# Half the depth of the mixing's output projection by Strassen's seven block products, in a two-layer decoder trunk

## The chip, the cores and the metric

The kernel runs on one core of one Trainium2 chip, as one launch. The time is device time in microseconds (us), lower is better; given is the median of several runs, and the runs of before agree within 0.01%. A profiled execution is a run of its own, with its own time.

## The reference

Two layers; in each a half-step SwiGLU block, a mixing of three attentions, and a second half-step SwiGLU block, each between RMSNorms. SEQ is 512, D_MODEL 1024, all in float32. The mixing ends with a product of two matrices, 512x1024 by 1024x1024:

```python
for l in range(DEPTH):                      # 2
    f = _swiglu(_rmsnorm(h, ffn1_pre_g[l]), ffn1_w_gate[l], ffn1_w_up[l], ffn1_w_down[l])
    h = h + 0.5 * _rmsnorm(f, ffn1_post_g[l])
    u = _rmsnorm(h, mix_pre_g[l])
    ...
    merged = (g_sb * (_merge_heads(o_sb) @ w_br_sb[l])
              + g_fx * (_merge_heads(o_fx) @ w_br_fox[l])
              + g_mem * (_merge_heads(o_mem) @ w_br_mem[l]))
    h = h + _rmsnorm(merged @ w_out[l], mix_post_g[l])
    f = _swiglu(_rmsnorm(h, ffn2_pre_g[l]), ffn2_w_gate[l], ffn2_w_up[l], ffn2_w_down[l])
    h = h + 0.5 * _rmsnorm(f, ffn2_post_g[l])
```

## The kernel before

**Numbers in two parts.** TensorE multiplies fp32r, a shortened float32. To keep float32's accuracy each operand is split into a high part (a cast on ScalarE, ACT, line 188) and a low part (what is left, on VectorE, DVE, line 189), and each product is three matmuls: high by high, low by high, high by low (`mm3`, lines 214 to 216). A matmul here multiplies a 128x128 piece by a 128x512 piece and adds into one PSUM bank of 128x512. A weight comes as a pair of row tiles: a load on SP's queue into a slot `raw_...` (line 262, 512 KB), the cast to `wh_...`, the low part `wl_...`.

**The SwiGLU blocks** use seven block products for eight (Strassen's scheme, in Winograd's variant) already. `block_units` makes the weights of the products. Three of the seven need sums of weight blocks: `BlockUnit.fetch` (L317) loads one block on SP and lets POOL issue a second DMA that adds the other block to it in SBUF; for products 3 and 6, `load` adds a further block on DVE (L343). The products' results are collected in three pairs of PSUM banks, and `product` hands them on: ACT copies a bank to the rows (L963), DVE adds a bank to them.

**The mixing** (`mixing`) works feature-major: `merge(br, ...)` forms a gate and a branch's projection for two of the eight 128-feature tiles at a time and adds them up in `merged` (tiles `mg`, four of 128x2x512). Its last four calls (branch 1, `dp` 0 to 3) finish two features tiles each, and split each at once into `ms_0` to `ms_7`, the left factors of the output projection.

**The output projection** is `down(w_out[l], ND, ...)`, with tiles named `wo` and `pwo`. It has 8 row tiles of weights (k-tiles) by 4 token tiles by 2 column halves by 3 passes, 192 matmuls a layer. `down` runs in this order: `first` does column half 0 of token tiles 0 and 1 side by side; `late` does half 1 of tile 0, then of tile 1; `second` half 1 of tiles 2 and 3; `late` half 0 of tile 2, then of tile 3. After each half `dst.result` takes the squares of the bank for the norm on ACT (`sq`, L554) and the scaled copy to the rows `f` on DVE (L559). When a tile is whole, `Q.spawn(dst.chain(t))` starts its chain: the norm (L505 to L510, on DVE and ACT), the addition to the residual `hm` (L596), the next norm, and at last four transposes per half on TensorE (`utb`, L613), whose results are the left factors of the next SwiGLU block. Its first weights (`tc`) are loaded in `first` too (`marks["next"]`).

**What sets the order.** The program is written through a queue of jobs, `Q`: a job is a list of weights to load and a generator that emits TensorE work, and `step` loads the weights of later jobs ahead (`AHEAD` = 4). Chains are woven into the jobs by a modelled clock (`PE_US`). The engines then take their instructions in the order in which they were written: each engine strictly in turn, and the loads in turn on SP's queue, the adding DMAs in turn on POOL's. With `carry=True`, which before only the SwiGLU blocks use, `down` seeds a bank with what stands in the rows already (`seed`, L1086, an ACT copy into PSUM), and its matmuls add to that:

```python
AFTER = {(0, 0): ((0, 1),), (0, 1): ((1, 1),), (1, 1): ((2, 1), (3, 1)), (2, 1): ((2, 0),), (2, 0): ((3, 0),)}
```

Of the kernel before, what the change touches and what calls it, by code (L numbers as in the profile page):

```python
# [9 lines left out]
F32 = mybir.dt.float32  # L10
# [3 lines left out]
ALU = mybir.AluOpType  # L14
# [3 lines left out]
P = 128  # L18
# [4 lines left out]
def kernel(  # L23
# [38 lines left out]
    nc = tc.nc  # L62
# [45 lines left out]
    def blk(tag, name):  # L108
        return stile([P, 2, S], tag, name)
# [525 lines left out]

    HR = 8 * ("o",)
    ORDER = (0, 2, 3, 4, 5, 1, 6)
    FIRST = (0, 1, 2, 3, 4, 5, 6)

    def ffn(l, src, wg, wu, wd, dst, name, spare, aside=None):  # L640

# [159 lines left out]
                for m in range(2):  # L801
                    hid[TG[-1] + 2 * b + m] = tuple(t[:, m] for t in both)

        def block_units(order, keep, rows, nm, src, pair=None, c0=0):

            before, made = st.get("units"), {}
            st["units"] = made
            for n in order:
                for k in range(0, rows, 2):
                    behind, twin = None, None  # L810
                    if n in (2, 5):
                        behind = made[n // 2 * 2 - 2 + n // 5, k] if before is None else before[4 if n == 2 else 5, k]
                    if n == 4 or n == 6 and order.index(1) == 5:
                        twin = made[n - 1 if n == 4 else 1, k]
                    made[n, k] = BlockUnit(n, src, rows, k, 2, S, keep, f"{nm}_{n}_{k}", pair, behind, twin)
                    made[n, k].c0 = c0
                yield n, [made[n, k] for k in range(0, rows, 2)]

        def group(f):

            order = FIRST if f == TG[0] else ORDER
            top = max((1, 4), key=order.index)
            keep = Keep(lambda i, k0: stile([P, 2, S], "v", f"kt{name}_{f}_{i}_{k0}", F32)[:])
            for n, uns in block_units(order, keep, ND // 2, f"t{name}_{f}", wg[l], (wg[l], wu[l]), f * P):
# [105 lines left out]

        SUM = (0, 1, 2, 0, 2, 0, 0)
        TO = ((0, 0), (0, 0), (1, 1), (0, 1), (0, 1), (1, 1), (1, 0))

        def product(ci, n, uns):
            if n == 0 and ci == 0:
                dst.begin()
# [30 lines left out]
        def products():  # L969

            def keeper(ci):
                def make(i, k0):
                    if k0 == 0:
                        st["bt", ci, i] = stile([P, 2, 2, S], ("k", "tri")[ci], f"bt{name}_{ci}_{i}", F32)
                    return st["bt", ci, i][:, k0 // 2]
                return Keep(make)

            last = st["units"]
            rounds = []
            for ci in range(NC):  # L980
                st["units"] = last
                rounds.append(dict(block_units(ORDER, keeper(ci), FC // 2, f"d{name}_{ci}", wd[l, ci * FC * P:(ci + 1) * FC * P])))
# [82 lines left out]
        down(wd[l, f0 * P:], NF - f0, hact, down_out, f"d{name}", dst, marks, reload, carry=True)  # L1065
        return marks

    def down(w, ktiles, act, emit, name, dst, marks, before=None, carry=False):

        PAIRS = ((0, 1), (2, 3))
        AFTER = {(0, 0): ((0, 1),), (0, 1): ((1, 1),), (1, 1): ((2, 1), (3, 1)), (2, 1): ((2, 0),), (2, 0): ((3, 0),)}
        banks = {}

        def seed(hf, ts):  # L1080

            for t, b in AFTER.get((ts[0], hf), ()) if carry else ():
                parts = HALVES if halves(b, t) else (FULL,)
                banks[t, b] = [pbank("mm", f"p{name}_{b}_{t}_{i}") for i in range(len(parts))]
                for pt, c in zip(banks[t, b], parts):
                    nc.scalar.activation(pt[:, c], dst.fs[t][:, HF[b]][:, c], AF.Copy, scale=-1.0 if b else 1.0)  # L1086

        def halves(hf, t):
            return t == NT - 1 and dst.g_pre is None and hf == 0

        def tiles(uns, hf, ts, done=None):
            seeded = (ts[0], hf) in banks
            pts = [banks.pop((t, hf))[0] if seeded else pbank("mm", f"p{name}_{hf}_{t}") for t in ts]
            for un in uns:
                for k in range(un.nk):
                    kk = un.k0 + k
                    for t, pt in zip(ts, pts):
                        ah, al = act(kk, slice(t * P, (t + 1) * P))
                        mm3(pt[:], ah, al, un.h[:, k], un.l[:, k], kk == 0 and not seeded, kk == ktiles - 1, seeded)
                        yield 3 * S * PE_US  # L1100
                    if kk == 1:
                        seed(hf, ts)
                if done is not None:
                    done()
            for t, src in [(t, emit(t, hf, pt[:], seeded)) for t, pt in zip(ts, pts)]:
                dst.result(t, hf, src)
# [24 lines left out]
        uns = [[Unit(w, k, 2, hf * S, S, f"{name}_{i}_{k}") for k in range(0, ktiles, 2)] for i, hf in enumerate((0, 1, 0))]  # L1131

        def first():
            for un in uns[1] + marks["next"][0]:
                un.load()
            if before is not None:
                before()
            dst.gains()
            yield from tiles(uns[0], 0, PAIRS[0])

        def second():

# [311 lines left out]
    def mixing(l, src, ks, vs, values, dst):  # L1454
# [105 lines left out]
        def merge(br, w_br, dp, apart=False):  # L1560
# [25 lines left out]
            def run():  # L1586
# [6 lines left out]
                for m in range(2):  # L1593
                    d = 2 * dp + m
                    nm = f"{l}_{br}_{d}"
                    a = gate[m]
                    pb = pbank("mm", "pb" + nm)
                    yield from gemm(pb[:], ub, m, list_act(st["o", br]))
                    md = st["merged"][d // 2][:, d % 2]
                    if br == 2:  # L1600
                        nc.vector.tensor_tensor(md, a[:], pb[:], ALU.mult)
                    else:
                        nc.vector.tensor_tensor(a[:], a[:], pb[:], ALU.mult)
                        nc.vector.tensor_tensor(md, md, a[:], ALU.add)
# [20 lines left out]
        for i, (br, _) in enumerate(heads):  # L1625
# [237 lines left out]
```

## Time and profile before

| | before |
|---|---|
| median of 3 runs | 2354.52 us (2354.39 to 2354.61) |
| the profiled execution | 2354.41 us |
| its span (first to last instruction) | 2352.7 us |
| granted TensorE clock, mean of the span | 0.999 |
| TensorE, matmul / weight load | 100% / 84% of the span |
| VectorE (DVE) | 76% |
| ScalarE (ACT) | 62% |
| GpSimd (POOL) | 9% |
| DMA queue q1 (SP's) | 305.76 MB, 40.2% of 16 engines' span |
| DMA queue q0 (POOL's) | 58.76 MB, 14.5% |

A row of the timeline has start and duration in us, engine, line of the code, operation, output<-inputs, and shapes. In a row of groups there stand a line, an engine, an operation and its tiles, the count, the busy time and the mean of one in ns, and then the idle time before the group's instructions and what ended it. A row of DMAs has the mean (or median) time from issue to landing at its end. Buffer numbers are left out of the names in the profile. The output projection of layer 0 starts at 802.62 us, that of layer 1 at 1968.05.

### The profile page before, as it was taken

The page shows a single profiled execution, that of the slowest core. Times are in us where ns is not written, and L with a number is a line of the kernel's source. Part 1 is how long each engine was busy: PE and PEld are TensorE (multiplying, and loading weights), DVE is VectorE, ACT ScalarE, POOL GpSimd, SP SyncE. Part 2 cuts the span into 40 slices and gives each one's busy share as a digit, 9 for nine tenths or more (in the row PEclk, how much of TensorE's full clock was granted, in tenths as well). Part 3 has the DMA queues.
Part 4 walks back from the last instruction along what each step waited for, and adds up shares of the span by engine and source line. Part 5 has one row for each costly group of instructions (what it writes and reads, how often), then busy time and mean ns, then how long its engine had stood idle before and what let it go on. Part 6 is the DMA issues. An engine that isn't in the chain of part 4 may idle for free.

```text
span 2352.7 us, 30543 instructions
## 1 busy us (share of the span) xinstructions
PE 2342.4 (100%) x11368; PEld 1970.4 (84%) x11368; DVE 1779.2 (76%) x2423; ACT 1453.0 (62%) x2347; POOL 213.4 (9%) x242
## 2 busy tenths in 40 slices
PE   9999999999999999999999999999999999999998
PEld 8888888888888888888888888888888888888887
DVE  8766977678776687768887679766877766866696
ACT  6665765576665565566665566656776655655574
POOL 1101100001120011101011110000011100111100
PEclk9999999999999999999999999999999999999999
DMA  8866854222323476659586767532222234776682
GB/s 249 234 180 173 230 181 142 72 73 81 88 66 116 153 221 173 179 158 258 174 215 170 187 186 232 190 101 81 72 82 81 72 126 153 223 182 176 179 224 98
DMA packets 233112, 366.46 MB, mean 156 GB/s; under 512 B 11242, under 2 KB 101634, under 8 KB 232452
## 3 DMA queue, kind: packets, MB, share of 16 engines
q1 hardware_dynamic: 202400, 305.76, 40.2%
q0 software_dynamic: 30560, 58.76, 14.5%
q8 instruction: 89, 1.46, 0.3%
q14 instruction: 59, 0.48, 0.1%
q10 hardware_dynamic: 4, 0.00, 0.0%
HBM read 349.80 MB, written 14.68 MB: 155 GB/s over the span
## 4 chain that ended last, share of the span: by engine, by line
PE 60%; DVE 0%; issue 0%; ACT 0%; DVEq 0%
PE ptc L214 5%; PE ptc L216 5%; PE ptc L215 5%; PE pdc L214 3%; PE pdc L216 3%; PE pdc L215 3%; PE pta L214 3%; PE pta L216 3%; PE pta L215 3%; PE pg L214 2%; PE pg L215 2%; PE pg L216 2%; PE pda L215 2%; PE pda L216 2%; PE pda L214 2%; PE pb L216 1%
## 5 line engine op out<-in xcount | busy, mean ns | idle before, releaser
L214 PE MATMUL pg<-us_a,wh_wg 128*128 128x512 f32 x384 | 150.9, 393 | 0.0
L216 PE MATMUL pg<-us_a,wl_wg 128*128 128x512 f32 x384 | 149.6, 390 | 0.0
L215 PE MATMUL pg<-us_a,wh_wg 128*128 128x512 f32 x384 | 149.5, 389 | 0.0
L189 DVE TENSOR_TENSOR wl_tc<-ktc,wh_tc 128x1024 fp32r<-128x1024 f32 x80 | 97.7, 1224 | 63.6 <-ACT wh_tc L188 63.6
L189 DVE TENSOR_TENSOR wl_ta<-kta,wh_ta 128x1024 fp32r<-128x1024 f32 x80 | 97.6, 1224 | 58.4 <-ACT wh_ta L188 58.4
L188 ACT CAST wh_tc<-ktc 128x1024 fp32r<-128x1024 f32 x80 | 84.1, 1054 | 68.0 <-PE ptc L216 47.8
L216 PE MATMUL pta<-wh_ta,aga 128*128 128x512 f32 x320 | 124.7, 390 | 1.2 <-DVE aga L189 1.2
L214 PE MATMUL ptc<-wh_tc,agc 128*128 128x512 f32 x320 | 125.4, 393 | 0.1
L214 PE MATMUL pta<-wh_ta,aga 128*128 128x512 f32 x320 | 125.2, 392 | 0.0
L216 PE MATMUL ptc<-wh_tc,agc 128*128 128x512 f32 x320 | 124.7, 390 | 0.0
L215 PE MATMUL ptc<-wl_tc,agc 128*128 128x512 f32 x320 | 124.6, 389 | 0.0
L188 ACT CAST wh_ta<-kta 128x1024 fp32r<-128x1024 f32 x80 | 84.2, 1053 | 65.5 <-PE pta L216 41.7
L215 PE MATMUL pta<-wl_ta,aga 128*128 128x512 f32 x320 | 124.6, 389 | 0.0
L189 DVE TENSOR_TENSOR wl_tc<-raw_tc,wh_tc 128x1024 fp32r<-128x1024 f32 x56 | 68.5, 1224 | 45.4 <-ACT wh_tc L188 45.4
L189 DVE TENSOR_TENSOR wl_ta<-raw_ta,wh_ta 128x1024 fp32r<-128x1024 f32 x58 | 70.9, 1224 | 42.0 <-ACT wh_ta L188 41.9
L188 ACT CAST wh_ta<-raw_ta 128x1024 fp32r<-128x1024 f32 x58 | 60.9, 1052 | 45.6 <-PE pta L216 38.0
L188 ACT CAST wh_tc<-raw_tc 128x1024 fp32r<-128x1024 f32 x56 | 59.0, 1054 | 48.1 <-PE ptc L216 36.6
L214 PE MATMUL ptc<-wh_tc,us_b 128*128 128x512 f32 x224 | 87.6, 391 | 0.2
L214 PE MATMUL pda<-wh_da,aa 128*128 128x512 f32 x224 | 87.5, 391 | 0.0
L214 PE MATMUL pdc<-wh_dc,ac 128*128 128x512 f32 x224 | 87.5, 391 | 0.0
L216 PE MATMUL ptc<-wh_tc,us_b 128*128 128x512 f32 x224 | 87.2, 389 | 0.0
L215 PE MATMUL ptc<-wl_tc,us_b 128*128 128x512 f32 x224 | 87.2, 389 | 0.0
(559 smaller groups left out, 7417.1 us busy)
## 6 DMA issues: line engine op xcount, KB each, us to landing
raw_wg<-in_w_gate_dram SPq DMA_DIRECT2D x48, 512.0 KB, 3.6
raw_ta<-in_ffn_w_gate_dram SPq DMA_DIRECT2D x44, 512.0 KB, 4.3
raw_tc<-in_ffn_w_gate_dram SPq DMA_DIRECT2D x44, 512.0 KB, 4.6
raw_da<-in_ffn_w_down_dram SPq DMA_DIRECT2D x42, 512.0 KB, 3.9
raw_dc<-in_ffn_w_down_dram SPq DMA_DIRECT2D x42, 512.0 KB, 3.9
kta<-in_ffn_w_up_dram SPq DMA_DIRECT2D x40, 512.0 KB, 6.1
ktc<-in_ffn_w_up_dram SPq DMA_DIRECT2D x40, 512.0 KB, 5.7
raw_wo<-in_w_out_dram SPq DMA_DIRECT2D x24, 512.0 KB, 3.7
```

Source lines behind the costliest of these rows:

```text
L188: both = [nc.scalar.copy(h_ap, src)]
L189: make = lambda: nc.vector.tensor_tensor(l_ap, src, h_ap.bitcast(F32), ALU.subtract)
L214: nc.tensor.matmul(pt, lh, rh, start=start, stop=False, skip_group_check=free)
L215: nc.tensor.matmul(pt, lh, rl, start=False, stop=False, skip_group_check=free)
L216: nc.tensor.matmul(pt, ll, rh, start=False, stop=stop, skip_group_check=free)
```

## The change

k-tiles 0 to 3, half of the depth, go by seven block products, and k-tiles 4 to 7 by `down` as before, which now starts from the products' sums. As blocks, the 512 tokens are two halves, the 512 rows of weights two halves of 256, and the 1024 columns two halves; a product has 2 k-tiles by 2 token tiles by 3 passes, 12 matmuls.

`factors` makes the left factors `ao` from `merged`, after `merge(1, ..., 1)` for products 0, 2, 3, 4 and after `merge(1, ..., 2)` for 5, 1, 6: four sums `so` on DVE and seven splits, for the four splits that made `ms_0` to `ms_3`. `out_product` multiplies; products 0, 3, 5, 6 share two PSUM banks (`pd_0`), 2 and 4 two others (`pd_2`), product 1 opens a third pair that ACT seeds from the rows. Behind a product its two banks are copied (ACT) or, for 4 and 5, added (DVE, L1699) to the rows `fb`; `out_sum` adds the banks of the first two halves in `down` to the rows (DVE, L1711). The sums of weight blocks `bo` come by SP's load and POOL's adding DMA.

Products 0, 2, 3, 4, 1 stand ahead of `down`. Products 5 and 6 are `middle`: jobs of `down` behind the late halves of tiles 0 and 1. `AHEAD` and the rest of `Q` stay. The diff, with `block_units` moved out of `ffn` and otherwise the same (it is given `st`):

```diff
+    ORDER_OUT = (0, 2, 3, 4, 1, 5, 6)
+    SUM = (0, 1, 2, 0, 2, 0, 0)
+    TO = ((0, 0), (0, 0), (1, 1), (0, 1), (0, 1), (1, 1), (1, 0))
...
-        def block_units(order, keep, rows, nm, src, pair=None, c0=0):
+    def block_units(st, order, keep, rows, nm, src, pair=None, c0=0):
...
-    def down(w, ktiles, act, emit, name, dst, marks, before=None, carry=False):
+    def down(w, ktiles, act, emit, name, dst, marks, before=None, carry=False, middle=()):
...
-                    if kk == 1:
+                    if kk == 1 and not (middle and (ts[0], hf) == (1, 1)):
                         seed(hf, ts)
...
         def first():
-            for un in uns[1] + marks["next"][0]:
+            for un in uns[1] + ([] if middle else marks["next"][0]):
                 un.load()
             if before is not None:
                 before()
             dst.gains()
-            yield from tiles(uns[0], 0, PAIRS[0])
+            ahead = iter([un for units, _ in middle for un in units])
+            yield from tiles(uns[0], 0, PAIRS[0], (lambda: next(ahead).load()) if middle else None)
+
+        def between(i, run):
+
+            if i == 0:
+                for un in marks["next"][0]:
+                    un.load()
+            yield from run()
+            if i == 0:
+                seed(1, (1,))
...
         for t in PAIRS[0]:
             Q.add(uns[1] if t == 0 else [], lambda t=t: late(uns[1], 1, t))
+        for i, (units, run) in enumerate(middle):
+            Q.add(units, lambda i=i, run=run: between(i, run))
         Q.add(marks["next"][0], second)
...
-                    if br == 1:
-                        mt = blk("v" if d < 4 else "qk"[d % 2], f"ms{l}_{d}")
+                    if br == 1 and d >= ND // 2:
+                        mt = blk("qk"[d % 2], f"ms{l}_{d}")
...
+        def factors(*ns):
+
+            for n in ns:
+                both = st["a", n] = stile([P, 2, 2, S // 2], "rs" if n == 6 else "v", f"ao{l}_{n}")
+                a = lambda i, j: st["merged"][j][:, :, HALVES[i]]
+                if n == 2:
+                    st["s"] = stile([P, 2, S // 2], "rs", f"so{l}", F32)[:]
+                sm = st.get("s")
+                if n == 2:
+                    nc.vector.tensor_tensor(sm, a(1, 1), a(1, 0), ALU.subtract)
+                elif n == 3:
+                    nc.vector.tensor_tensor(sm, sm, a(0, 0), ALU.add)
+                elif n == 4:
+                    nc.vector.tensor_tensor(sm, sm, a(0, 1), ALU.subtract)
+                elif n == 5:
+                    nc.vector.tensor_tensor(sm, a(0, 0), a(1, 0), ALU.subtract)
+                from_ = a(*((0, 0), (0, 1), None, None, None, None, (1, 1))[n]) if n in (0, 1, 6) else sm
+                split(both[:, 0], both[:, 1], from_, scale=-1.0 if n == 3 else None)
+
         for dp in range(ND // 2):
             merge(1, w_br_fox, dp, apart=dp == 0)
+            if dp == 1:
+                Q.add([], lambda: iter(factors(0, 2, 3, 4) or ()))
+            if dp == 2:
+                Q.add([], lambda: iter(factors(5, 1, 6) or ()))
...
-            dst.begin()
             new_h(f"m{l}")
...
-        down(w_out[l], ND, lambda k, c=FULL: list_act(st["ms"])(k, c), lambda t, hf, pt, last: pt, f"wo{l}", dst, marks, reload)
+        def out_product(n, uns):
+
+            if n == 0:
+                dst.begin()
+            if n in (0, 2):
+                st["b", SUM[n]] = [pbank("z", f"pd{l}_{n}_{e}") for e in range(2)]
+            pts = st["b", SUM[n]]
+            for un in uns:
+                for k in range(un.nk):
+                    for e in range(2):
+                        c = slice(e * P, (e + 1) * P)
+                        mm3(pts[e][:], st["a", n][:, 0, k, c], st["a", n][:, 1, k, c], un.h[:, k], un.l[:, k],
+                            n in (0, 2) and k == 0, n in (1, 4, 6) and k == un.nk - 1, free=True)
+                        yield 3 * S * PE_US
+            i, hf = TO[n]
+            for e in range(2):
+                f = dst.fs[2 * i + e][:, HF[hf]]
+                if n in (4, 5):
+                    nc.vector.tensor_tensor(f, f, pts[e][:], ALU.add)
+                else:
+                    nc.scalar.copy(f, pts[e][:])
+            if n == 4:
+                st["b", 1] = [pbank("z", f"pd{l}_1_{e}") for e in range(2)]
+                for e in range(2):
+                    nc.scalar.copy(st["b", 1][e][:], dst.fs[e][:, HF[0]])
+
+        def out_sum(t, hf, pt, seeded):
+            if seeded:
+                return pt
+            f = dst.fs[t][:, HF[hf]]
+            nc.vector.tensor_tensor(f, f, pt, ALU.add)
+            return f
+
+        keep = Keep(lambda i, k0: stile([P, 2, S], "tri", f"bo{l}_{i}", F32)[:])
+        middle = []
+        for n, uns in block_units({}, ORDER_OUT, keep, 2, f"o{l}", w_out[l, 0:ND // 2 * P]):
+            job = uns, lambda n=n, uns=uns: out_product(n, uns)
+            if n in (5, 6):
+                middle.append(job)
+            else:
+                Q.add(*job)
+        down(w_out[l, ND // 2 * P:], ND // 2, lambda k, c=FULL: list_act(st["ms"])(k, c), out_sum, f"wo{l}", dst, marks, reload,
+             carry=True, middle=middle)
```

**TensorE, behind the late half of tile 1**, where `second` (tiles 2 and 3) began at once before (`pwo_1_2` is column half 1 of token tile 2):

```order
L216 MATMUL pwo_1_1_7422<-wh_wo_1_6_7274,ms_7_7253 128x512
L214 MATMUL pwo_1_2_7457<-wh_wo_1_0_7256,ms_0_6899 128x512
L215 MATMUL pwo_1_2_7457<-wl_wo_1_0_7257,ms_0_6899 128x512
L216 MATMUL pwo_1_2_7457<-wh_wo_1_0_7256,ms_0_6899 128x512
L214 MATMUL pwo_1_3_7458<-wh_wo_1_0_7256,ms_0_6899 128x512
```

Now (of product 5 the last three rows):

```order
L214 MATMUL pd_0_1_7284<-wh_o_5_0_7385,ao_5_7147 128x512
L215 MATMUL pd_0_1_7284<-wl_o_5_0_7386,ao_5_7147 128x512
L216 MATMUL pd_0_1_7284<-wh_o_5_0_7385,ao_5_7147 128x512
L214 MATMUL pd_0_0_7283<-wh_o_6_0_7390,ao_6_7154 128x512
L215 MATMUL pd_0_0_7283<-wl_o_6_0_7391,ao_6_7154 128x512
L216 MATMUL pd_0_0_7283<-wh_o_6_0_7390,ao_6_7154 128x512
L214 MATMUL pwo_1_2_0_7522<-wh_wo_1_0_7341,ms_4_7126 128x512
L215 MATMUL pwo_1_2_0_7522<-wl_wo_1_0_7342,ms_4_7126 128x512
L216 MATMUL pwo_1_2_0_7522<-wh_wo_1_0_7341,ms_4_7126 128x512
L214 MATMUL pd_0_1_7284<-wh_o_6_0_7390,ao_6_7154 128x512
```

Products 5 and 6 stand between tile 1's late half and tiles 2 and 3, and share the banks `pd_0_0` and `pd_0_1`; product 6 comes bank by bank, six matmuls each, with three of tile 2 between.

**DVE, the same stretch.** Before (`fb_0` is the row of token tile 0, `gpb` the gain, `nfb` and `nhb` the small sums of the norms, `w_tc` the next block's weights):

```order
L189 TENSOR_TENSOR wl_wo_1_6_7275<-raw_wo_1_6_7058,wh_wo_1_6_7274 128x1024
L189 TENSOR_TENSOR w_tc_0_0_2_7285<-raw_tc_0_0_2_7266,w_tc_0_0_2_7285 128x1024
L559 SCALAR_TENSOR_TENSOR fb_1_7291<-pwo_0_1_7315,gpb_7302 128x512
L559 SCALAR_TENSOR_TENSOR fb_0_7290<-pwo_1_0_7394,gpb_7302 128x512
L505 TENSOR_SCALAR nfb_0_7306<-nfb_0_7306 128x1
L509 SCALAR_TENSOR_TENSOR nfb_0_7306<-nfb_0_7306 128x1
```

Now:

```order
L189 TENSOR_TENSOR wl_o_6_0_7391<-bo_0_7044,wh_o_6_0_7390 128x1024
L559 SCALAR_TENSOR_TENSOR fb_0_7279<-fb_0_7279,gpb_7404 128x512
L559 SCALAR_TENSOR_TENSOR fb_1_7280<-fb_1_7280,gpb_7404 128x512
L189 TENSOR_TENSOR w_tc_0_0_0_7452<-raw_tc_0_0_0_7309,w_tc_0_0_0_7452 128x1024
L189 TENSOR_TENSOR w_tc_0_0_2_7457<-raw_tc_0_0_2_7345,w_tc_0_0_2_7457 128x1024
L559 SCALAR_TENSOR_TENSOR fb_0_7279<-pwo_1_0_0_7430,gpb_7404 128x512
L505 TENSOR_SCALAR nfb_0_7408<-nfb_0_7408 128x1
L559 SCALAR_TENSOR_TENSOR fb_1_7280<-pwo_1_1_0_7468,gpb_7404 128x512
L509 SCALAR_TENSOR_TENSOR nfb_0_7408<-nfb_0_7408 128x1
L505 TENSOR_SCALAR nfb_1_7409<-nfb_1_7409 128x1
L510 SCALAR_TENSOR_TENSOR nfb_0_7408<-nfb_0_7408 128x1
L1699 TENSOR_TENSOR fb_2_7281<-fb_2_7281,pd_0_0_7283 128x512
```

Directly ahead of these stand `wl_o_5` (L189) and the two sums of L1711, so the last row, the addition of product 5's first bank, has fourteen rows ahead of it from `wl_o_5` on; behind it come tile 0's L596, a small row of tile 1's norm and the addition of the second bank.

**SP's queue.** Before:

```order
L262 DMA raw_wo_1_0_7040<-in_w_out_dram 128x2x512
L262 DMA raw_wo_1_2_7046<-in_w_out_dram 128x2x512
L262 DMA raw_wo_1_4_7052<-in_w_out_dram 128x2x512
L262 DMA raw_wo_1_6_7058<-in_w_out_dram 128x2x512
L317 DMA raw_tc_0_0_0_7260<-in_ffn_w_gate_dram 128x2x512
```

Now:

```order
L262 DMA raw_wo_1_0_7170<-in_w_out_dram 128x2x512
L136 DMA gpb_7404<-in_mix_post_g_dram 128x1024
L262 DMA raw_wo_1_2_7274<-in_w_out_dram 128x2x512
L317 DMA bo_1_7276<-in_w_out_dram 128x2x512
L317 DMA raw_o_6_0_7303<-in_w_out_dram 128x2x512
L136 DMA gqb_7406<-in_ffn_pre_g_dram 128x1024
L317 DMA raw_tc_0_0_0_7309<-in_ffn_w_gate_dram 128x2x512
```

The load of the sum `bo_1` (for product 5) stands behind `raw_wo_1_2`; POOL's queue has the adding DMAs of `bo_0` and `bo_1` in addition. TensorE has 10775 rows before and 10751 now, DVE 2364 and 2396, ACT 2136 and 2180, SP 568 in both, POOL 221 and 225.

More of the change, by code (lines that the diff above doesn't have):

```diff
@@ L637 @@
     ORDER = (0, 2, 3, 4, 5, 1, 6)
+    ORDER_OUT = (0, 2, 3, 4, 1, 5, 6)
+    SUM = (0, 1, 2, 0, 2, 0, 0)
+    TO = ((0, 0), (0, 0), (1, 1), (0, 1), (0, 1), (1, 1), (1, 0))
     FIRST = (0, 1, 2, 3, 4, 5, 6)
+    def block_units(st, order, keep, rows, nm, src, pair=None, c0=0):
+        before, made = st.get("units"), {}
+        st["units"] = made
+        for n in order:
+            for k in range(0, rows, 2):
+                behind, twin = None, None
+                if n in (2, 5):
+                    behind = made[n // 2 * 2 - 2 + n // 5, k] if before is None else before[4 if n == 2 else 5, k]
+                if n == 4 or n == 6 and order.index(1) == 5:
+                    twin = made[n - 1 if n == 4 else 1, k]
+                made[n, k] = BlockUnit(n, src, rows, k, 2, S, keep, f"{nm}_{n}_{k}", pair, behind, twin)
+                made[n, k].c0 = c0
+            yield n, [made[n, k] for k in range(0, rows, 2)]
     def ffn(l, src, wg, wu, wd, dst, name, spare, aside=None):
@@ L802, in last_hidden @@
                     hid[TG[-1] + 2 * b + m] = tuple(t[:, m] for t in both)
-        def block_units(order, keep, rows, nm, src, pair=None, c0=0):
[L806 to L817, printed above, removed]
         def group(f):
@@ L823, in group @@
             keep = Keep(lambda i, k0: stile([P, 2, S], "v", f"kt{name}_{f}_{i}_{k0}", F32)[:])
-            for n, uns in block_units(order, keep, ND // 2, f"t{name}_{f}", wg[l], (wg[l], wu[l]), f * P):
+            for n, uns in block_units(st, order, keep, ND // 2, f"t{name}_{f}", wg[l], (wg[l], wu[l]), f * P):
                 yield uns, (lambda n=n, uns=uns: gate_up(f, n, uns, top))
@@ L929, in first_factor @@
                 split(h[:, two], l[:, two], from_, scale=-1.0 if n == 3 else None)
-        SUM = (0, 1, 2, 0, 2, 0, 0)
-        TO = ((0, 0), (0, 0), (1, 1), (0, 1), (0, 1), (1, 1), (1, 0))
         def product(ci, n, uns):
@@ L981, in products @@
                 st["units"] = last
-                rounds.append(dict(block_units(ORDER, keeper(ci), FC // 2, f"d{name}_{ci}", wd[l, ci * FC * P:(ci + 1) * FC * P])))
+                rounds.append(dict(block_units(st, ORDER, keeper(ci), FC // 2, f"d{name}_{ci}", wd[l, ci * FC * P:(ci + 1) * FC * P])))
             for n, ci in DOWN:
```

## Prediction

> **What bounds the kernel now.** I read the page's first part, then TensorE's waits, then the two stretches that hold the output projection.
>
> ```profile
> span 2352.7 us, 30543 instructions
> PE 2342.4 (100%) x11368; PEld 1970.4 (84%) x11368; DVE 1779.2 (76%) x2423; ACT 1453.0 (62%) x2347; POOL 213.4 (9%) x242
> PEclk9999999999999999999999999999999999999999
> engine line waited for: us in total, times, longest us
> PE warm L1733 <- DVE warm L1817: 1.3, 1, 1.3
> PE pta L216 <- DVE aga L189: 1.2, 1, 1.2
> PE ptf L1291 <- DVE pf L1362: 0.7, 2, 0.4
> ```
>
> TensorE is busy from end to end at the full granted clock; all its waits come to 3.2 us, and none lies in the projection. So a matmul that goes is time won, and a wait that comes on TensorE is time lost, one for one.
>
> ```profile
> 802.62 0.39 PE L214 MATMUL pwo<-wh_wo,ms 128*128 128x512 f32 x1
> ...
> 813.27 0.39 PE L216 MATMUL pwo<-wh_wo,ms 128*128 128x512 f32 x1
> 813.50 0.39 PE L214 MATMUL pwo<-wh_wo,ms 128*128 128x512 f32 x1
> L214 PE MATMUL pwo<-wh_wo,ms x128: 389/389/476, 802.6 to 2012.7; 128*128 128x512 f32 x128
> ```
>
> The first 48 matmuls of layer 0's projection start from 802.62 to 813.27 and the 49th at 813.50: 10.88/48 = 0.2267 us each. (The 0.39 of a row is the time to the end of a pipelined matmul.) The group has 3 x 128 = 384 in both layers.
>
> **What goes.** Seven products of 12 matmuls (2 k-tiles, 2 token tiles, 3 passes) stand for half the depth, which took 4 x 2 x 4 x 3 = 96. That is 12 fewer a layer, 24 in all, and the built order agrees: 10775 rows on TensorE before, 10751 now. 24 x 0.2267 = 5.44 us; the profiled execution took 2354.41 (span 2352.7 and 1.7 around it), so without a new wait it would take 2348.97, and 2349.1 against the median of 2354.52, which is 0.1 above it. Everything else is the question of what TensorE must now wait for.
>
> **Work added beside TensorE.**
>
> ```profile
> 770.00:780.00 10.00, 10.00 (x46) 8.28 (x45) 5.64 (x8) 4.68 (x7) 0.00 (x0) 1.00 0.44 161
> 780.00:790.00 10.00, 10.00 (x46) 8.29 (x45) 7.02 (x10) 5.09 (x7) 0.00 (x0) 1.00 0.36 105
> 802.60:848.30 45.70, 45.70 (x211) 38.02 (x210) 34.92 (x50) 26.67 (x50) 0.00 (x0) 1.00 0.55 175
> 814.39 0.68 DVE L559 SCALAR_TENSOR_TENSOR fb<-pwo,gpb 128x512 f32<-128x512 f32 x1
> 814.99 1.22 DVE L189 TENSOR_TENSOR wl_wo<-raw_wo,wh_wo 128x1024 fp32r<-128x1024 f32 x1
> 816.12 1.22 DVE L189 TENSOR_TENSOR w_tc<-raw_tc,w_tc 128x1024 fp32r<-128x1024 f32 x1
> L963 ACT COPY fc<-pdc 128x512 f32<-128x512 f32 x20 | 11.6, 582 | 5.2 <-PE pdc L216 5.2
> ```
>
> (Columns of the windows: stretch, length, then busy time of PE, weight load, DVE, ACT, POOL, the clock, the DMA share.) Issued back to back, DVE starts the next row 0.60 us after a 512-wide one and 1.14 after a 1024-wide one. The factors are 7 splits and 4 sums where 4 splits were: 7 more DVE rows, 4.2 us, and 3 ACT casts, in 770 to 790, where DVE worked 12.7 of 20 us and ACT 9.8. That is hidden by idle DVE time; without this cover the gates of the last two merges would be late by up to those 4.2 us. In the projection itself ACT gets 10 copies of product banks and 8 seeds at 0.58 each (10.4 us) and one more weight cast; DVE one more weight low part, two 1.22 sums, six bank additions (four of products, two of the first rows), about 7.2 us. Both fit into the 45.7 us in sum. What matters is order: both engines work through their queues strictly in turn, so I followed the handovers to TensorE by hand, the start of matmul n at 802.62 + 0.2267 n.
>
> ```profile
> 811.02 1.05 ACT L188 CAST wh_wo<-raw_wo 128x1024 fp32r<-128x1024 f32 x1 [1.67 <-PE pwo L216]
> 811.98 1.05 ACT L188 CAST w_tc<-raw_tc 128x1024 fp32r<-128x1024 f32 x1
> 813.02 0.60 ACT L554 ACTIVATE sqb<-pwo 128x512 f32<-128x512 f32 x1
> 813.51 0.20 ACT L554 ACTIVATION_READ_ACCUMULATOR sqb<-pwo 128x1 f32 x1
> 804.00 1.22 DVE L189 TENSOR_TENSOR wl_wo<-raw_wo,wh_wo 128x1024 fp32r<-128x1024 f32 x1
> 805.13 0.69 DVE L1604 TENSOR_TENSOR mg<-mg,ga 128x512 f32<-128x512 f32 x1
> ```
>
> A reader of a bank starts 0.42 to 0.45 after the start of its last matmul (813.02 against the 812.60 of matmul 44, tile 0's last), ACT's next row 0.95 after a 1024-wide cast and 0.5 after a 512-wide copy.
>
> The copy of product 0's second bank ends by 807.6, and product 3 wants the bank at 808.74. The seeds of product 1: its place is matmul 56, at 815.31, because eight matmuls of the first rows were put ahead of it; ACT's queue holds wh_wo_1_0, which waits for product 4's last weight (matmul 47, 813.27 + 0.45), and then the seed: 813.72 + 0.95 + 0.58 = 815.25. It fits, barely; I take nothing, up to 0.3 if I am late by a little.
>
> Product 6 is the place that does not fit. It uses product 5's two banks, and starts directly behind it, at matmul 120: 829.82. Bank 0 has its last matmul at 828.91, DVE could add it from 829.33; but the addition stands on DVE behind a run that begins with wl_o_5: four 1024-wide rows (wl_o_5, wl_o_6, two of w_tc), six 512-wide ones and four small ones.
>
> ```profile
> 820.47 0.20 DVE L505 TENSOR_SCALAR nfb<-nfb 128x1 f32<-128x1 f32 x1
> 821.18 0.22 DVE L509 SCALAR_TENSOR_TENSOR nfb<-nfb 128x1 f32<-128x1 f32 x1 [0.51 <-ACT nfb L507]
> 821.43 0.16 DVE L510 SCALAR_TENSOR_TENSOR nfb<-nfb 128x1 f32<-128x1 f32 x1
> 821.63 1.28 DVE L596 SCALAR_TENSOR_TENSOR hm<-fb,nfb,hm 128x1024 f32<-128x1024 f32 x1
> L764 DVE TENSOR_TENSOR cc<-cc,ptc 128x512 f32<-128x512 f32 x40 | 25.6, 681 | 0.0
> ```
>
> 4 x 1.14 + 6 x 0.60 + 0.85 = 9.0 us, and 0.68 for the addition itself. wl_o_5 follows ACT's cast wh_o_5. ACT comes to that cast at 819.7: wh_wo_1_2 waits for product 1's last matmul (number 67, 817.81 + 0.45 = 818.26), 0.95, a copy 0.5. If the weight sum were there, the cast would end at 820.8, the run at 829.8, the addition at 830.5, and TensorE would wait 0.7 us. That is the lower bound of this wait. (The other bank's addition, the 1.28 row and a small one later, meets TensorE just in time, since six matmuls and three of the next rows lie between.)
>
> **The block sum** bo_1 is what can be late: one load on SP, then an adding DMA on POOL, then the cast.
>
> ```profile
> raw_wo<-in_w_out_dram SPq DMA_DIRECT2D x1, 512.0 KB, 4.5
> raw_wo<-in_w_out_dram SPq DMA_DIRECT2D x1, 512.0 KB, 5.2
> ktc<-in_ffn_w_up_dram SPq DMA_DIRECT2D x2, 512.0 KB, 7.2
> 848.28 1.01 SPq L317 DMA_DIRECT2D ktc<-in_ffn_w_up_dram  x2
> 856.18 1.19 POOL L317 DMA_DIRECT2D ktc<-in_ffn_w_gate_dram  x1 [148.15 <-DMA ktc<-in_ffn_w_up_dram]
> ktc<-in_ffn_w_gate_dram POOLq DMA_DIRECT2D x1, 512.0 KB, 6.6
> DMA to landing us min/median/max: 6.0/11.7/14.6
> ```
>
> On SP it stands behind raw_wo_1_2, which waits until wl_o_1 has read the slot. The last gate's sum (805.13 before) now has wl_o_4 ahead of it and wl_o_1 behind: 805.13 + 1.14 + 0.60 + 1.22 = 808.1; one issue later (0.5, half of the two in the SP row) bo_1 goes out, 808.6. Loads issued among others took 4.5 and 5.2 us (SP, 814 to 817); 4.8 gives 813.4. POOL issued 0.7 after such a landing (848.28 + 7.2 = 855.5; 856.18): 814.1. The nearest adding DMA landed after 6.6: 820.7. So wh_o_5 starts 1.0 late, the run with it, and TensorE waits 1.7 us at product 6, in each layer: the second layer's queues have the same rows. Bounds of the landing, from the issue on POOL: from below, any landing by 819.7 (5.6) costs the 0.7; from above, the slowest of the sums of the down projections, load and add together (last row), took 14.6, 8 us more than I take, and its median 11.7. I take 6.6, since the DMA share of 0.55 here is below that of the stages in which those stand.
>
> The page "DMA: Bandwidth & Descriptors" of the Trainium skill, section "Anatomy of one DMA — SWDGE (gpsimd) path", fits a POOL-issued DMA as 2.0 us plus bytes/436e3; that would be an estimated 3.2 us for these 512 KB, and the sum would be the 2350.5 of the rival below. The 6.6 of the row speaks against it for a DMA that adds.
>
> **Later.** The transposes of tiles 0 and 1 come more than 12 us after their last matmul, and tile 2's stand 76 rows behind its own, as before; the next block's weights have slack of several us. I cost these at nothing; a late adding DMA would shift them all.
>
> **Sum.** 2 x (12 x 0.2267 - 1.7) = 2.0 us less: 2352.4 for the profiled execution, **2352.5** against the median, 0.09% faster. A change of 0.2%, 4.7 us, is about what a measurement of this kernel tells from none.
>
> **Rivals.** (1) *The sum lands in time*, so DVE's run alone counts: 0.7 a layer, 2354.5 - 5.4 + 1.4 = 2350.5. For it: POOL has nothing else here. Against: the fastest load and sum of the down projections together took 6.0 (the minimum of the last row above), and the nearest sum alone 6.6, where 5.6 is needed. (2) *All handovers fit*: DVE's run is shorter by half a microsecond or TensorE's other work starts it earlier; at most 0.2 a layer is left, 2349.1 to 2349.8. Against it: 9 us of rows in 8.5 us of matmuls. (3) *The adding DMA is late and blocks ACT*: ACT waits at wh_o_5, and behind it in its queue stand wh_o_6, the squares of tiles 0 and 1, the next block's casts and the seeds of tiles 2 and 3. With the median of 11.7, 5.1 us later, the wait is 6.8 a layer and the time 2354.5 + 2 x (6.8 - 2.72) = 2362.7. It costs more than is won from a landing 7.6 us after issue, and over 0.2% from 10.0. The same could befall bo_0 ahead of product 2, where about 1 us of slack absorbs it. For it: the page's median for such DMAs is above 7. Against: they run there in pairs. That the matmuls don't go is excluded by the rows.
>
> ```profile
> ktc<-in_ffn_w_gate_dram POOLq DMA_DIRECT2D x20, 512.0 KB, 7.3
> btc<-in_ffn_w_down_dram POOLq DMA_DIRECT2D x16, 512.0 KB, 8.3
> ```
>
> **How the numbers follow.** Forecast 0.34 (its own range 2350.9 to 2354.4), rival 1 0.20, rival 2 0.20, rival 3 0.26, of which 0.19 is above 2359.2. Faster by over 0.2% is rival 2: 0.20; slower by over 0.2%: 0.19; within: 0.61. The range 2348.6 to 2360.0 leaves out about 0.18 of rival 3; below, it reaches half a microsecond under the 2349.1 of no wait at all, since some of the 3.2 us that TensorE waits elsewhere could shift too.
>
> **What would show it.** Right: on the page of the changed kernel TensorE's waits grow by some 3.4 us, in two waits of pd<-ao (L214) on DVE's fb (the addition behind product 5), about 1.7 each; ACT idle before wh_o<-bo, released by the adding DMA, for about 1 us; 24 matmuls fewer at the same 0.2267. Rival 1: no such idle time of ACT, waits of 0.7. Rival 2: no wait of pd. Rival 3: waits of over 2.7 a layer, and the DMA named at wh_o. Wrong in another way: a wait at product 1 on ACT's seed, at product 3 or 4 on a copy, or at the transposes utb.

## The result, and the profile after

| | before | after |
|---|---|---|
| median | 2354.44 us (2353.78 to 2354.61, 6 runs) | 2366.44 us (2365.29 to 2368.13, 6 runs) |
| ratio | | 1.0051, 95% interval 1.0038 to 1.0064 |
| the profiled execution, its span | 2354.41, 2352.7 us | 2368.13, 2366.4 us |

The change is 12 us slower, beyond the range of the prediction and beyond its slow rival's 2362.7. First the page's first part of the changed kernel and TensorE's waits:

```profile
span 2366.4 us, 30587 instructions
PE 2340.7 (99%) x11344; PEld 1967.8 (83%) x11344; DVE 1800.2 (76%) x2455; ACT 1473.0 (62%) x2391; POOL 218.7 (9%) x246
engine line waited for: us in total, times, longest us
PE pd L214 <- DVE fb L1699: 10.7, 2, 5.3
PE pd L214 <- ACT fb L1701: 2.0, 2, 1.0
...
PE pd L215 <- DVE wl_o L189: 0.8, 2, 0.6
```

24 matmuls have gone (11368 to 11344), and in the projection three waits have come, each once a layer (what lies between the lines is elsewhere in the program). By far the largest is the one that was forecast, of product 6 on DVE's addition of product 5 (L1699): 5.3 us a layer, not 1.7. The second, of product 3 on ACT's copy of product 0 (L1701), was to be nothing. Then the projection of layer 0, its first and last matmul before and now:

```profile
847.70 0.39 PE L216 MATMUL pwo<-wh_wo,ms 128*128 128x512 f32 x1
```

```profile
802.17 0.39 PE L214 MATMUL pd<-wh_o,ao 128*128 128x512 f32 x1
...
831.00 0.39 PE L216 MATMUL pd<-wh_o,ao 128*128 128x512 f32 x1
836.74 0.76 PE L214 MATMUL pd<-wh_o,ao 128*128 128x512 f32 x1 [5.34 <-DVE fb L1699]
837.30 0.63 PE L215 MATMUL pd<-wl_o,ao 128*128 128x512 f32 x1
837.73 0.63 PE L216 MATMUL pd<-wh_o,ao 128*128 128x512 f32 x1
...
853.67 0.39 PE L216 MATMUL pwo<-wh_wo,ms 128*128 128x512 f32 x1
```

From the first start to the last it took 45.08 us before (802.62 to 847.70) and 51.50 now, where 12 matmuls fewer should make 42.36. Layer 1 took 53.03 (1973.65 to 2026.68). So the projections cost 6.42 and 7.95 more than before, 14.4 in all; the span grew by 13.7. (The profiled execution was the longest of the six, 1.7 us above their median, so the parts below come to somewhat more than the 12 us of the medians.) Of layer 0's 9.1 us above 42.36, the gap ahead of product 6 is 5.51 (836.74 - 831.00 - 0.23), the one at product 3 is 1.13, the low part of product 5 costs 0.36, and about 2.1 lie in matmuls that are slow: behind the long wait they follow each other at 0.43 us and not at 0.23 (837.30 and 837.73). (The expectations below also count a "ramp": the few tenths of a us that the first matmuls behind a wait take longer.) The windows give the granted clock of that stretch (columns as in the prediction's windows):

```profile
802.17:853.67 51.50, 44.99 (x196) 36.16 (x195) 39.48 (x56) 36.42 (x67) 1.20 (x1) 0.93 0.58 185
836.70:840.50 3.80, 3.76 (x9) 3.01 (x10) 3.80 (x6) 3.80 (x8) 0.00 (x0) 0.53 0.66 241
2008.60:2014.00 5.40, 5.33 (x13) 4.22 (x14) 5.40 (x8) 5.40 (x11) 0.00 (x0) 0.50 0.62 220
```

8 matmuls in layer 0 (the last of the row's nine is back at 0.24) and 13 in layer 1 run at about half the clock. The page "TensorE: Matmul & The Clock Gate" of the Trainium skill, section "What's actually happening" in Part 1, has TensorE at half its clock after an idle window of about 3.4 us, until it has been busy for a window of that length. The same page of the Trainium skill, section "Wait — 56ns, not 53.3ns?", has 426.7 ns for a 512-wide matmul at that clock. These rows agree with the 0.43 us, and the slow stretches, 3.6 us (836.74 to 840.29) and 5.7 us (2008.67 to 2014.35), are as long as that window or longer.

What the waits go back to stands in the chain of waits, followed back from 845 us (start, length, and what it is):

```profile
783.93 4.87 DMA bo<-in_w_out_dram
...
789.47 7.26 DMA bo<-in_w_out_dram
...
796.82 1.06 ACT wh_o L188
...
804.08 0.70 DVE mg L1616
...
807.55 0.69 DVE mg L1616
808.24 1.15 DVE wl_o L189
...
809.82 6.81 DMA bo<-in_w_out_dram
...
817.30 8.86 DMA bo<-in_w_out_dram
...
826.24 1.06 ACT wh_o L188
...
827.33 0.99 DVE wl_o L189
...
835.99 0.61 DVE fb L1699
836.74 0.76 PE pd L214
```

It is one chain, and both sums are in it. bo_0, the sum for product 2, is loaded (4.87) and added (7.26); ACT's cast of it comes late, then the last gate and merge (mg), then `wl_o_1`, which frees the slot that SP needs before it comes to bo_1; its load (6.81) and its adding DMA (8.86) follow, then the cast `wh_o_5` and DVE's run to the addition. On ACT's timeline the two sums are its long idle times:

```profile
796.82 1.05 ACT L188 CAST wh_o<-bo 128x1024 fp32r<-128x1024 f32 x1 [3.42 <-DMA bo<-in_w_out_dram]
...
808.27 0.62 ACT L188 CAST ms<-mg 128x512 fp32r<-128x512 f32 x1 [0.47 <-DVE mg L1616]
808.80 1.07 ACT L1701 COPY fb<-pd 128x512 f32<-128x512 f32 x2
...
826.24 2.00 ACT L188 CAST wh_o<-bo 128x1024 fp32r<-128x1024 f32 x2 [5.55 <-DMA bo<-in_w_out_dram]
```

The copy of product 0's second bank (first of the two at 808.80) stands behind the last cast of `ms`, which waited for the last merge; product 3 wanted it at 808.30 and got it at 809.43.

### The profile page after: what moved, and what is told of

Same layout as the page of the kernel before. It is cut to its first block, busy times and chain, and to the rows that moved or that the text cites. A ratio compares the mean times of both kernels' runs of the same rounds, so it can differ in the third digit from the quotient of the medians.

```text
span 2366.4 us, 30587 instructions
## 1 busy us (share of the span) xinstructions
PE 2340.7 (99%) x11344; PEld 1967.8 (83%) x11344; DVE 1800.2 (76%) x2455; ACT 1473.0 (62%) x2391; POOL 218.7 (9%) x246
## 4 chain that ended last, share of the span: by engine, by line
PE 93%; DVE 2%; DMA 2%; ACT 1%; issue 1%; POOL 0%; SPq 0%; DVEq 0%; ACTq 0%; POOLq 0%
PE ptc L214 5%; PE ptc L215 5%; PE ptc L216 5%; PE pta L214 5%; PE pta L216 5%; PE pta L215 5%; PE pg L214 3%; PE pg L215 3%; PE pg L216 3%; PE pdc L214 3%; PE pdc L215 3%; PE pdc L216 3%; PE pda L215 3%; PE pda L216 3%; PE pda L214 3%; DMA bo<-in_w_out_dram 2%
## 5 line engine op out<-in xcount | busy, mean ns | idle before, releaser
L189 DVE TENSOR_TENSOR wl_tc<-ktc,wh_tc 128x1024 fp32r<-128x1024 f32 x80 | 97.7, 1223 | 63.9 <-ACT wh_tc L188 63.8
L189 DVE TENSOR_TENSOR wl_ta<-kta,wh_ta 128x1024 fp32r<-128x1024 f32 x80 | 97.5, 1222 | 57.7 <-ACT wh_ta L188 57.7
L189 DVE TENSOR_TENSOR wl_ta<-raw_ta,wh_ta 128x1024 fp32r<-128x1024 f32 x58 | 70.8, 1223 | 43.3 <-ACT wh_ta L188 43.1
L189 DVE TENSOR_TENSOR wl_tc<-raw_tc,wh_tc 128x1024 fp32r<-128x1024 f32 x56 | 68.5, 1223 | 41.5 <-ACT wh_tc L188 41.5
L214 PE MATMUL pda<-wh_da,aa 128*128 128x512 f32 x224 | 87.5, 391 | 0.0
L216 PE MATMUL pda<-wh_da,aa 128*128 128x512 f32 x224 | 87.2, 389 | 0.0
L215 PE MATMUL pda<-wl_da,aa 128*128 128x512 f32 x224 | 87.2, 389 | 0.0
```

The source lines that it names most:

```text
L189: make = lambda: nc.vector.tensor_tensor(l_ap, src, h_ap.bitcast(F32), ALU.subtract)
L214: nc.tensor.matmul(pt, lh, rh, start=start, stop=False, skip_group_check=free)
L215: nc.tensor.matmul(pt, lh, rl, start=False, stop=False, skip_group_check=free)
L216: nc.tensor.matmul(pt, ll, rh, start=False, stop=stop, skip_group_check=free)
```

## The experiments

Each kernel is the changed kernel with the edit shown or named. The ratio is to the kernel before.

**1. The second sum issued earlier.** The fetch of product 5's weights (SP's load and POOL's adding DMA) is called behind the second set of factors; all other rows of ACT, DVE and TensorE keep their order.

```diff
             if dp == 2:
-                Q.add([], lambda: iter(factors(5, 1, 6) or ()))
+                Q.add([], lambda: iter(factors(5, 1, 6) or [un.fetch() for un in middle[0][0]] and ()))
```

> Only the load and the adding DMA of bo_1 are issued some 20 us earlier (behind the second set of factors). Theory A (the late sum holds ACT, and so DVE's run to product 5's addition): bo_1 is there when ACT comes to wh_o_5 at about 820.6, DVE's run of 9.0 us starts at 821.7, product 6 waits about 0.5 instead of 5.5, the cast and low part of product 5 cost no 0.36, and no slow matmuls follow (1.75). 2 x 7.1 less than the 2366.4: about 2352. Rival B (the run on DVE alone keeps the wait, the DMA is cover): the wait at product 6 stays above 3 us and the time above 2360.

Measured: 2354.15 us (2353.28 to 2356.26), ratio 1.0000, 0.999 to 1.0009: 12.3 us less than the change, as much as the change had lost. TensorE's waits of this kernel:

```profile
PE pd L214 <- ACT fb L1701: 3.1, 2, 1.6
...
PE pd L214 <- DVE fb L1699: 0.4, 2, 0.2
```

The wait at product 6 is 0.2 a layer, no matmul runs at half the clock, and the wait at product 3 has grown from 1.0 to 1.6, as bo_0's adding DMA, with bo_1's load beside it, took 8.2 us here and not 7.3. So DVE's run, of which 0.7 was forecast as the least wait, is not too long; the late sum is what holds it. Rival B is out.

**2. The same, and product 5 ahead of tile 1's late half.**

```diff
         for t in PAIRS[0]:
             Q.add(uns[1] if t == 0 else [], lambda t=t: late(uns[1], 1, t))
-        for i, (units, run) in enumerate(middle):
-            Q.add(units, lambda i=i, run=run: between(i, run))
+            for i, (units, run) in enumerate(middle):
+                if i == t:
+                    Q.add(units, lambda i=i, run=run: between(i, run))
```

> As the early sum, and product 5 stands behind tile 0's late half, product 6 behind tile 1's, so that 12 matmuls (2.7 us) lie between. Theory A: no wait is left at product 6; what remains is the wait at product 3 (1.1 and a slower ramp of 0.2 a layer): 2349.1 + 2 x 1.3 = 2351.7. Rival B (DVE's run is what is too long whatever stands where): a wait of over 2 us moves to tile 2 or product 6, time above 2354.5.

Measured: 2353.73 us (2352.77 to 2356.24), ratio 0.9997, 0.9988 to 1.0006. No wait at product 6 is left, and 3.1 us at product 3; the time is 2.0 above the forecast, since the waits at product 3 are 0.6 longer each, and in the profiled execution layer 0's is followed by seven matmuls at 0.43. Between this kernel and the first one the runs can't tell.

**3. The wait filled with matmuls that nothing reads.** They go into a free bank of PSUM.

```diff
             if i == 0:
                 seed(1, (1,))
+                fill = pbank("z", f"fill{name}")
+                for j in range(24):
+                    ah, al = act(0, slice(0, P))
+                    tc.keep_in_program_order(nc.tensor.matmul(fill[:], ah, middle[0][0][0].h[:, 0], start=j == 0, stop=j == 23))
```

> 24 matmuls that nothing reads stand between products 5 and 6 (24 x 0.2267 = 5.4 us), in the time that TensorE waits there. Theory C (the nine matmuls at 0.43 behind the wait are slow because TensorE stood still for 5.5 us): none is slow, the granted clock of 800 to 850 stays at 0.99 or more, 1.75 a layer come back: about 2363. Rival D (they are slow for another cause, such as DVE or DMA work beside them): the slow matmuls stay, time 2366 or more.

Measured: 2366.16 us (2365.26 to 2367.07), ratio 1.0050, 1.0035 to 1.0065: the time is that of the change, and the forecast of 2363 missed. What was asked of the clock came out: the stretch behind the filling, and TensorE's rows there:

```profile
838.40:842.40 4.00, 3.99 (x17) 3.31 (x18) 3.57 (x6) 4.00 (x10) 0.00 (x0) 1.00 0.74 237
```

```profile
831.19 5.60 PE L1153 MATMUL fillwo<-wh_o,ms 128*128 128x512 f32 x24
837.11 0.40 PE L216 MATMUL pd<-wh_o,ao 128*128 128x512 f32 x1
838.41 0.51 PE L214 MATMUL pd<-wh_o,ao 128*128 128x512 f32 x1 [0.91 <-DVE fb L1703]
```

The clock is 1.00, and no matmul is slow in either layer. But the edit also moved product 6: its banks now take turns, with no rows of tile 2 between, so that after three matmuls it waits for the addition of the second bank as well, 1.07 us more (837.11 to 838.41, less 0.23). That gives back about half of what the full clock saves (1.7 us in layer 0, 2.7 in layer 1). In the profiled executions the two projections took 50.05 and 51.52, 3.0 less than the change's; the medians don't show it. That the slow matmuls come of TensorE's standing still is borne out by the clock; how much of the 12 us they are can't be read from this kernel's time.

**4. All seven products ahead of the rows.**

```diff
-            if n in (5, 6):
+            if n in ():
                 middle.append(job)
```

> Products 5 and 6 stand ahead of the projection's rows, none behind tiles 0 and 1. Theory A: bo_1 is loaded two places earlier on SP and the run on DVE ahead of product 5's addition is short (no rows of tiles 0 and 1 in it), so no wait above 1 us at product 6: 2350 to 2355. Rival E (their place is not what costs: DMA adding lands late wherever they stand): waits of over 3 us a layer at product 5 or 6, time above 2358.

Measured: 2360.28 us (2358.41 to 2363.88), ratio 1.0028, 1.0017 to 1.0039. As theory A had it, no wait stands at product 6; the number still missed, since product 3 waited longer than in the change (3.5 in sum, not 2.0) and waits came that nobody had forecast, at the transposes of tiles 0 and 1 and the first matmuls behind them:

```profile
PE pd L214 <- ACT fb L1701: 3.5, 2, 2.0
PE utb L613 <- DVE nhb L503: 1.4, 2, 1.0
PE utb L613 <- DVE fb L603: 1.4, 2, 0.7
```

The chains of tiles 0 and 1 need the time that products 5 and 6 fill when they stand behind them. With them ahead, the next block comes too early for its factors.

**5. The first sum issued earlier, the second as in the change.** bo_0's fetch is called behind the first merge of branch 1.

```diff
+        sums = {}
         for dp in range(ND // 2):
             merge(1, w_br_fox, dp, apart=dp == 0)
+            if dp == 0:
+                Q.add([], lambda: iter(sums[2].fetch() or ()))
...
+            sums[n] = uns[0]
             job = uns, lambda n=n, uns=uns: out_product(n, uns)
```

> Only bo_0, the sum for product 2, is loaded and added earlier (some 14 us); bo_1 stands where the change has it. Theory F (product 3 waits because ACT stood at wh_o_2 for bo_0's adding DMA, 3.4 us, and so came late to the last gates, to ms_7's cast and to the copies of product 0): ACT doesn't wait for bo there, the wait at product 3 (1.1 and 0.2 of ramp a layer) goes, and bo_1 goes out about 2 us earlier since wl_o_1 frees its slot earlier; product 6 still waits, about 4.5. 2366.4 - 2 x (1.3 + 0.9) = about 2362. Rival G (product 3 waits because ACT has too many rows there, whatever the sums do): its wait stays above 0.8 and the time at 2365 to 2367.

Measured: 2357.14 us (2356.01 to 2358.8), ratio 1.0011, 1.0002 to 1.0021. The wait at product 3 is gone, as theory F said; the time is 5 us under the forecast, since layer 1 fared far better at product 6 than layer 0. TensorE and ACT of this kernel, layer 0 ahead (its wait at product 6 was 4.5) and layer 1 behind:

```profile
823.60 2.00 ACT L188 CAST wh_o<-bo 128x1024 fp32r<-128x1024 f32 x2 [4.25 <-DMA bo<-in_w_out_dram]
1989.73 2.00 ACT L188 CAST wh_o<-bo 128x1024 fp32r<-128x1024 f32 x2 [1.52 <-DMA bo<-in_w_out_dram]
```

```profile
2000.23 0.47 PE L214 MATMUL pd<-wh_o,ao 128*128 128x512 f32 x1 [1.80 <-DVE fb L1702]
```

The adding DMA took 9.1 us in layer 0 and 7.0 in layer 1, with the same rows around it. Layer 0's projection took 2.7 us less than in the change (48.83), near the forecast, and layer 1's 6.8 less (46.19). Where the DMA took 7.0, near the 6.6 of the prediction, the wait is 1.8, near its 1.7.

**6. Both sums earlier.** The edits of 5 and of 1 (as `sums[5].fetch()`).

> Both sums early, everything else as in the change, the order on TensorE, ACT and DVE too. Theories A and F: no wait above 0.3 a layer in the projection; the early second sum took 2354.2 with 3.1 of waits at product 3 and about 0.6 of ramps; without them about 2350.5, and not under the 2349.1 of 24 matmuls fewer and no wait. Rival G: 2354.

Measured: 2350.07 us (2349.52 to 2351.23, 11 runs; before 2354.5), ratio 0.9981, 0.9972 to 0.999. The order on TensorE, ACT and DVE is that of the change; only two loads and two adding DMAs a layer are issued earlier, and 16.4 us have gone against the change. Its waits in the projection are 0.2 a layer:

```profile
PE pd L214 <- DVE fb L1702: 0.4, 2, 0.2
```

**7. Both sums earlier, and product 5 ahead of tile 1's late half.** The edits of 6 and 2.

> Both sums early, product 5 behind tile 0's late half and product 6 behind tile 1's. Theory A: the last 0.2 a layer at product 6 goes too: 2350.1. Rival: what is moved ahead of tile 1's half delays tile 1's chain by 2.7 us, and a wait at its transposes takes the gain: 2351 or more.

Measured: 2349.40 us (2348.71 to 2350.0, 11 runs), ratio 0.9978, 0.997 to 0.9987, the fastest of all. No wait of `pd` is left, and the projection's window is busy throughout:

```profile
803.00:845.45 42.45, 42.45 (x197) 35.19 (x196) 35.95 (x52) 35.48 (x67) 0.00 (x0) 1.00 0.66 211
1965.56:2008.04 42.48, 42.48 (x197) 35.17 (x195) 35.95 (x52) 35.46 (x67) 0.00 (x0) 1.00 0.66 210
```

45.08 less 12 x 0.2267 is 42.36. Tile 1's chain, 2.7 us later, makes nothing wait.

**8. The second sum in its place, added by DVE.** Its second block comes by a plain load into a slot of `raw` right behind the first, and DVE adds the two; the adding DMA of it is gone.

```diff
...
-                tc.keep_in_program_order(self.block(t, two, accum_op=ALU.add))
+                if not self.plain:
+                    tc.keep_in_program_order(self.block(t, two, accum_op=ALU.add))
...
-                self.block(self.raw[:], self.BLOCKS[self.n])
+                self.block(self.raw[:], two if self.plain else self.BLOCKS[self.n])
...
+                if self.plain:
+                    nc.vector.tensor_tensor(src, src, self.raw[:], ALU.add)
...
+            uns[0].plain = n == 5
```

> bo_1 is issued where the change issues it, but its second block comes by a plain load on SP into a raw slot, and DVE adds the two (one more 1.22 row); POOL's adding DMA for it is gone. Theory H (the 8.9 us of the adding DMA behind the load are what makes the sum late, not the late issue alone): both loads land by about 819, ACT finds the sum ready when it comes to wh_o_5 at 820.6 or a little later, product 6 waits 0.5 to 1.5 instead of 5.5 and no slow matmuls follow; product 3's wait stays at 1.1: 2353 to 2356. Rival I (any second transfer issued there lands as late, because of the loads around it): a wait of over 3.5 us a layer stays, 2361 or more.

Measured: 2354.41 us (2353.87 to 2357.25), ratio 1.0002, 0.9992 to 1.0011: 12 us less than the change, with the same late issue.

```profile
PE pd L214 <- DVE fb L1702: 3.0, 2, 1.5
PE pd L214 <- ACT fb L1704: 2.2, 2, 1.1
```

ACT no longer stands at `wh_o_5`: the second transfer, sent right behind the first, is there in time. The 1.5 us that are left come of DVE. It adds bo_1's two blocks (L343), and then product 6's sum (L346), whose load now stands behind one more load; it waits for both, ahead of `wl_o_5`, which starts at 823.52 though its cast is ready at 822.15:

```profile
818.70 1.23 DVE L343 TENSOR_TENSOR bo<-bo,raw_o 128x1024 f32<-128x1024 f32 x1 [1.36 <-DMA raw_o<-in_w_out_dram]
821.25 1.23 DVE L346 TENSOR_TENSOR bo<-bo,raw_o 128x1024 f32<-128x1024 f32 x1 [1.32 <-DMA raw_o<-in_w_out_dram]
```

In the change the second transfer started when the first had landed, through POOL and as an adding DMA, and TensorE waited 5.3. Which of the three made it late this run doesn't tell apart.

## Why the prediction was wrong

**The matmuls** were right: 24 fewer, at 0.2267 each. Experiment 7 has the 2349.1 that the sum gives without a wait, within its runs.

**The place and the mechanism** were right: the one large wait is at product 6, on the addition behind DVE's run, which follows `wl_o_5`, `wh_o_5` and bo_1's adding DMA. The run took 8.7 us (827.33 to 835.99 in the chain) where 9.0 was worked out.

**The size failed first at the sum's landing**, "813.4 [...] 814.1 [...] 820.7": it was 826.16. Of the 5.5 us, 1.2 are the issue (809.82, not 808.6), 2.0 the load (6.81, not 4.8) and 2.3 the adding DMA (8.86, not 6.6; 9.2 in layer 1). The 6.6 came from one row in another stage, chosen "since the DMA share of 0.55 here is below that of the stages in which those stand". A share averaged over 46 us says nothing of the 15 in which the sum is under way: in the changed kernel it is 0.58 over the projection, but 1.00 while bo_1's adding DMA runs (the last figure but one of a window's row):

```profile
817.30:826.16 8.86, 8.86 (x41) 7.33 (x40) 2.45 (x2) 2.45 (x4) 1.20 (x1) 1.00 1.00 303
```

SP's timeline has a burst there (a row of two has its second issue at its end):

```profile
788.74 19.29 SPq L262 DMA_DIRECT2D raw_wo<-in_w_out_dram  x2
...
819.23 2.64 SPq L262 DMA_DIRECT2D raw_wo<-in_w_out_dram  x2
```

From the second of the first row (807.66) to the second of the last (821.50) SP issues ten DMAs, bo_1 the fourth of them. With less beside it, bo_1's adding DMA in experiment 6 took 5.6 in layer 0, at a share of 0.59 (its window, then its row of DMAs), and 6.1 in layer 1:

```profile
794.35:800.00 5.65, 5.65 (x27) 4.68 (x26) 4.11 (x5) 3.62 (x5) 1.20 (x1) 1.00 0.59 96
bo<-in_w_out_dram POOLq DMA_DIRECT2D x1, 512.0 KB, 5.6
```

With a sum 5.5 us late the prediction's own chain gives a wait of 7.2. It was 5.3 (5.5 from matmul to matmul), since two things made up for the rest: the waits ahead had TensorE come to product 6 only at 831.2, 1.4 later than the 829.82 of the prediction, and DVE's run was 0.3 shorter.

The bound from above was wrong as well. The row with 6.0, 11.7 and 14.6 was read as load and add together; its times are of single DMAs, loads and adds alike, so that the pair takes well more (the 6.0 that rival 1 has for both together is the same misreading). From issue to sum bo_1 took 16.3 us (809.82 to 826.16), over the 14.6 that was to be the most.

**A term that was set to nothing failed second**: bo_0, "where about 1 us of slack absorbs it". Product 2 did have the time, but ACT did not: it stood 3.42 us at `wh_o_2`, with the last gates, the last `ms` cast and product 0's copies queued behind. That cost the 1.0 at product 3, and bo_1's late issue. Experiment 5 shows both: without it there is no wait at product 3, and bo_1 is issued at 807.84, ahead of the 808.6 of the prediction.

**Third, a price was missing**: the half clock behind a long wait. The 8 and 13 slow matmuls took 1.7 and 2.7 us more than at full speed in the profiled execution (3.55 us against 8 x 0.2267, and 5.68 against 13 x 0.2267), and this appears in none of the prediction's cases. Rival 3 had the mechanism of the largest wait and the sign. It came to 2362.7 and not to 2366.4, although its wait of 6.8 was longer than the one measured, for want of the wait at product 3 and of the slow matmuls. Its chance of 0.26 was too low: beside the single 6.6 the trace had medians of 7.3 and 8.3 for such DMAs over the whole program, and of 11.7 in the stretch of the row that was misread.

**What remains open**: how much each of the loads around it adds to the adding DMA, and what sets 9.1 in one layer and 7.0 in the other with the same rows. It is not the layer, as in experiment 3 it was 7.7 in layer 0 and 9.9 in layer 1; nor is it the DMA share alone, which was 0.97 or more in all four. No run changes those loads alone. That the burst is what makes the DMA slow is therefore argued from the shares, not shown.

## What to carry to other kernels

A block product saves matmuls only if the sums it needs are there when an in-order engine comes to their cast: issue the load and the adding DMA one or two stages ahead, and don't price two chained transfers by their best row. A plain load right behind the first, with the addition on DVE, is another way: in experiment 8 it took as much off the change as the earlier issue of experiment 1. Where ACT stands at a late transfer, list everything queued behind it, and price that too; "the product itself has slack" is not enough. And price a wait of several us on TensorE at more than its length: behind each wait of 4.5 to 5.3 us here the next 7 to 13 matmuls ran at half the clock.

## What the runs showed of the hardware

The half clock doesn't need a wait as long as 5 us: in experiment 2, layer 0, seven matmuls in a row at 0.43 (the first and the second of them below) followed a wait of 1.6 us, while experiment 1's waits of the same length were followed by none. Seven more followed the wait of 1.8 us in experiment 5, layer 1, and none the wait of 2.0 in experiment 4.

```profile
810.65 0.50 PE L214 MATMUL pd<-wh_o,ao 128*128 128x512 f32 x1 [1.56 <-ACT fb L1702]
...
811.59 0.63 PE L214 MATMUL pd<-wh_o,ao 128*128 128x512 f32 x1
812.01 0.63 PE L215 MATMUL pd<-wl_o,ao 128*128 128x512 f32 x1
```

By these rows a wait of under 2 us can do it, though not each one does. The page "TensorE: Matmul & The Clock Gate" of the Trainium skill, section "What's actually happening" in Part 1, has an idle window of about 3.4 us for the fall of the clock; these waits are shorter.

The adding DMAs of bo_0 and bo_1, of 512 KB, took 5.6 us at the least and 9.9 at the most in these runs (experiment 6, layer 0, and experiment 3, layer 1), against 3.8 for a plain load of the same size (the median of experiment 6's six loads of raw_wo from 780 to 830) and 6.8 for bo_1's plain load in the burst of the change.
